# Output projections in two passes of half the contraction, six of eight tiles of each pass by Strassen's seven products

## The chip, the cores and the metric

The kernel runs on one core of a Trainium2 chip. The metric is device time in microseconds (us) from the start to the end of one execution. Engines are named as in the profile: PE is TensorE (matmuls), DVE is VectorE, ACT is ScalarE, POOL is GpSimd, SP is SyncE, whose queue issues nearly all DMAs here.

## The reference

One step of a two-layer trunk on a prompt of 1024 rows and 8 sample rows, which share the weights; the kernel computes all 1032 rows as columns of one matrix. Layer 0 is HGRN2, layer 1 a causal chunked gMLP. What matters here is the output projection at each layer's end, `y`, of a contraction over D_INNER = 2048 to D_MODEL = 1024:

```python
def hgrn2_mixer(h, s0, w_in, lb, g_norm, w_out):
    ...
    o = rmsnorm(o, g_norm).reshape(B, L, D_INNER).astype(h.dtype)
    return (o * jax.nn.silu(z)) @ w_out, S

def chunk_mlp_mixer(h, w_in, ln_g, ln_b, w_sp, b_sp, w_out):
    ...
    y = (u * s * jax.nn.silu(z)) @ w_out
    return y, v_tail

    for i in range(DEPTH):
        ...
        h = h + y
        gate = jax.nn.sigmoid(rmsnorm(h, norm_ple[i]) @ w_ple_gate[i])
        h = h + gate * (p[i] @ w_ple_proj[i])
```

## The kernel before

The 1032 columns are held transposed (features on the 128 partitions) in three chunks c = 0, 1, 2 of W = 384, 384 and 264 columns. A float32 product is made of three float32r matmuls in `mm3` (L217 to L221): high part times high part, high times low, low times high. Every operand is therefore split: ACT casts the value to its high part ("hi"), and DVE or POOL subtracts that from the value ("lo"); `split` (L213) does it for data (lo at L215), `split_weights` for weights (lo at L147). In tile names, `bh` and `bl` are the hi and lo parts of the activations (in the code also `hh`, `hl`), `whi` and `wlo` those of a weight tile, `shi` and `slo` those of sums of weight quarters (`ssum`).

The output projection is `out_phase`. Its operand is the gated branch, 16 blocks of 128 rows, which the stage ahead has stored block by block in DRAM (`ozd`); its first eight blocks lie split in SBUF when the phase starts, the second eight are loaded again and split by `load_zt` (into tiles that the profile calls zh and zl). It makes eight tiles m of 128 output rows, and for each tile and chunk one PSUM group (`ps_o`) over all 16 blocks, in two halves hf of eight (`out_half`). `add` then has DVE add the group to the residual h (L911, rows `hr[c][m]`, called h in the profile), ACT square it, and POOL sum the squares for the next normalisation (L255). The residual is loaded two tiles ahead (`load_h`, L878).

Weights come in the order of the list `order`; `take` hands out a tile and has `load` prepare the next, so that a weight tile is cast and subtracted one ahead.

Layer 1's input projection (between the two phases) already uses Strassen's form in `unit`: two weight tiles of 128 output rows against chunks 0 and 1, contraction split in two, are 2 x 2 quarters on either side, so seven products of 4 blocks x 3 matmuls at 384 columns do for eight. `load_unit` loads the two weight tiles and builds the four sums of their quarters on POOL (L188, L190, L193, L195), each split by ACT and DVE; `mix` forms the sums and differences of the operand's quarters. Chunk 2 is done plainly within the unit (`last`). The products' results are combined by DVE from PSUM into u2, u4 and c22.

Just ahead of layer 1's output projection stands a fill: `pple` multiplies half of the per-layer embedding into PSUM groups `ps_pple`, which ACT copies (L338) to SBUF on their way to DRAM (`ppd`), while the last unit's outputs are gated and stored. Its last rows of gating are `sg` (ACT L1270, DVE L1271) and `s` (POOL L1264, the product with u).

The order of PE's work is the order of the program. DVE, ACT, POOL and SP are ordered by a scheduler from priorities (`tc.high_priority`, PRI), constraints (`tc.issue_after`) and the program's order; `tk.tick()` advances side processes (normalisation, mixing) between groups of matmuls. A scratch tile named `tmp` has four buffers.

Of the kernel before, what the change touches and what calls it, by code (L numbers as in the profile page):

```python
# [17 lines left out]
P = 128  # L18
# [14 lines left out]
ZQ = 7  # L33
FDEL = ((2, 2), (2, 2), (1, 3))
# [46 lines left out]
def trunk_kernel(ctx, tc, xT, st, pT, nrm, wina, lbl, gna, wouta, winb, lng, lnb, lngr, lnbr,  # L81
# [38 lines left out]

    order = [("p", 0, 0)]
    for h in range(NH):
# [3 lines left out]
    half_order = [(m, f) for q in range(0, KT, 2) for m, f in  # L126
                  (((q, 0), (q + 1, 0), (q, 1), (q + 1, 1)) if q == 0 else
                   ((q, 0), (q, 1), (q + 1, 0), (q + 1, 1)))]
    order += [("oa", m, f) for m, f in half_order]
# [6 lines left out]
    order += [("ob", m, f) for m, f in half_order]  # L136
# [25 lines left out]
    def load(n, wait=False):  # L162
        if n >= len(order) or n in loaded or wait and order[n][0] == "B":
            return
        if order[n][0] == "B":
            loaded[n] = load_unit(order[n][1])
# [7 lines left out]
    def load_unit(m):  # L174
# [8 lines left out]
        for i in range(2):  # L183
            nc.sync.dma_start(a[i], winb[m + i])
# [161 lines left out]
    def load_zt(zt, parts, stage, n=2, lag=0, tie=True):  # L346


        todo = [(c, k0, k) for c, k0 in parts for k in range(0, zt[c, k0][2], n)]
        stg = []  # L350
        def fetch(i):
            if i < len(todo):
                c, k0, k = todo[i]
                stg.append(stage(W[c]))
                last["zt"] = nc.sync.dma_start(stg[i], ozd[c][:, k0 + k:k0 + k + n, :])

        for i in range(len(todo) + lag):
            if not lag:
                fetch(i)
            if i >= lag:  # L360
                c, k0, k = todo[i - lag]
                zh, zl, _ = zt[c, k0]
                hi = A.copy(zh[:, k:k + n, :], stg[i - lag])
                if tie:
                    tc.keep_in_program_order(hi)
                V.tensor_tensor(zl[:, k:k + n, :], stg[i - lag], zh[:, k:k + n, :].bitcast(F32), ALU.subtract)
# [15 lines left out]
    def out_half(ps, wt, zt, c, hf):  # L382
        for k in range(8):
# [3 lines left out]
                hf == 0 and k == 0, hf == 1 and k == 7)  # L387
# [461 lines left out]
    sA.close()  # L849

# [16 lines left out]
    def out_phase(key, zt, ssq, first, done, pre, parts, late, fill=None):  # L867

        with ExitStack() as s:
            st = stage2(pool(s, "zstg"), 3)  # L870
            zp = pool(s, "oz")

            def load_h(m):
                if m < KT:
                    src = xT[:, m] if first else hd[m]
                    with tc.issue_after(last["zt"].ins):
                        for c in CH:
                            nc.sync.dma_start(hr[c][m], src[:, OFF[c]:OFF[c] + W[c]])  # L878

            for c, k0, nk in parts:  # L880
                zt[c, k0] = (zp.tile([P, nk, W[c]], F32R, name=f"zh{c}_{k0}"),
                             zp.tile([P, nk, W[c]], F32R, name=f"zl{c}_{k0}"), nk)
            if fill:

                to = itertools.cycle([hr[c][m] for c in (2, 0) for m in range(4)])
                more = load_zt(zt, late[0], one(lambda: next(to)), 1, 8)
                todo = load_zt(zt, late[1], st, 2, 3)
                for gen, n in ((more, 8), (todo, 3)):
                    for _ in range(n):
                        next(gen)  # L890
                for _ in fill:
                    tk.tick()
                for _ in range(8):
                    next(more)
                run(todo)
                run(more)
            else:
                run(load_zt(zt, late, st, tie=False))
            for m in range(4):
                load_h(m)  # L900
# [4 lines left out]
            def half(ps, wt, c, hf):  # L905
                for _ in out_half(ps, wt, zt, c, hf):
                    tk.tick()

            def add(m, c, ps):
                with tc.high_priority(offset=PRI if m == KT - 1 else 0):  # L910
                    V.tensor_tensor(hr[c][m], hr[c][m], ps[:, :W[c]], ALU.add)  # L911
                accum_sq(sp, ssq[c], hr[c][m], m == 0, m == KT - 1, W[c])
                if m == KT - 1:
                    done(c)


            wt = pre["w"] if pre else take(key, 0, 0)
            for c in CH:
                if c not in pre:
                    pre[c] = bank()  # L920
                    half(pre[c], wt, c, 0)
            wt = take(key, 1, 0)
            pre1 = [pp.tile([P, 384], F32, name="ps_o1", tag=t, bufs=1) for t in ("pA", "po", "pt")]
            for c in CH:
                half(pre1[c], wt, c, 0)
            for m, pm in ((0, pre), (1, pre1)):
                wt = take(key, m, 1)
                for c in CH:
                    half(pm[c], wt, c, 1)
                    add(m, c, pm[c])  # L930
            for m in range(2, KT):
                wts = [take(key, m, hf) for hf in range(2)]
                load_h(m + 2)
                for c in CH:
                    ps = bank()
                    for hf in range(2):
                        half(ps, wts[hf], c, hf)
                    add(m, c, ps)
# [41 lines left out]
    act = new_act()  # L980
# [454 lines left out]
```

## Time and profile before

| | us |
|---|---|
| median of 3 runs (lowest to highest) | 1914.62 (1912.47 to 1915.26) |
| the profiled execution | 1914.28 |
| its span in the profile | 1912.4 |
| PE busy | 1882.9 |
| DVE, ACT, POOL busy | 1156.3, 800.1, 432.8 |
| first output projection, first to last matmul on `ps_o` | 766.45 to 947.96, 181.51 long |
| second | 1620.94 to 1802.45, 181.51 long |

The span is what the profile covers of one execution; the 1.9 us between it and the execution's time lie outside. The mean granted clock of PE is 0.993. Busy times of different engines overlap: PE's says how much of the span is matmul, the others' say how full the engines are that feed it.

### The profile page before, as it was taken

To read this page: it belongs to the slowest core of one execution; us is meant where nothing else is said; L and a number is where in the kernel's file an instruction comes from. 1 tells how busy PE (TensorE), PEld (TensorE's weight loads), DVE (VectorE), ACT (ScalarE), POOL (GpSimd) and SP (SyncE) were. 2 spreads that over 40 slices of the span, in tenths; PEclk is the share of its full clock that TensorE was granted. 3 is DMA by queue.
4 is the path that set the end of the run, shared out by engine and by line. 5 is a ranking of instruction groups with operands and counts; after the bars stand their busy time and mean duration, and the time that the engine had idled before them with its cause. 6 is when DMAs were issued, how large, how long until landed. Compare 5 with 4: busy or idle time off the path is not lost.

```text
span 1912.4 us, 33713 instructions
## 1 busy us (share of the span) xinstructions
PE 1882.9 (98%) x13250; PEld 1856.2 (97%) x13250; DVE 1156.3 (60%) x2610; ACT 800.1 (42%) x1711; POOL 432.8 (23%) x441
## 2 busy tenths in 40 slices
PE   9999999999999999999999999999999999999997
PEld 8999999999999998999999999999999999999997
DVE  5967676766767677411465755577777776311455
ACT  6463544444454546311244544434434335311342
POOL 4110000000010001011233332345445451011321
PEclk8999999999999999999999999999999999999998
DMA  6231323222231326711243343323333236611123
GB/s 214 76 117 61 118 72 103 78 81 78 92 99 60 111 69 191 251 49 51 76 143 117 109 145 99 90 81 106 124 114 106 97 108 197 222 45 45 67 89 111
DMA packets 124302, 203.76 MB, mean 107 GB/s; under 512 B 11568, under 2 KB 97264, under 8 KB 123120
## 3 DMA queue, kind: packets, MB, share of 16 engines
q1 hardware_dynamic: 124144, 201.61, 32.2%
q8 instruction: 104, 1.70, 0.4%
q14 instruction: 54, 0.44, 0.1%
HBM read 148.75 MB, written 52.82 MB: 105 GB/s over the span
## 4 chain that ended last, share of the span: by engine, by line
PE 90%; DVE 5%; DMA 2%; POOL 1%; ACT 1%; issue 1%; SPq 0%; DVEq 0%; ACTq 0%; POOLq 0%
PE ps_proj L219 18%; PE ps_proj L221 18%; PE ps_proj L220 18%; PE ps_o L219 6%; PE ps_o L220 6%; PE ps_o L221 6%; PE ps_d L221 1%; PE ps_d L219 1%; PE ps_d L220 1%; PE psp L1255 1%; PE pC L672 1%; PE pt_o L718 1%; PE p L638 1%; PE pt_g L1061 1%; PE pss L269 1%
## 5 line engine op out<-in xcount | busy, mean ns | idle before, releaser
L219 PE MATMUL ps_proj<-bh,whi 128*128 128x384 f32 (+1 forms) x2160 | 695.1, 322 | 2.1 <-ACT pple_t L338 1.6
L221 PE MATMUL ps_proj<-bh,wlo 128*128 128x384 f32 (+1 forms) x2160 | 679.9, 315 | 0.5 <-DVE wlo L147 0.5
L220 PE MATMUL ps_proj<-bl,whi 128*128 128x384 f32 (+1 forms) x2160 | 678.8, 314 | 1.4 <-POOL bl L215 1.4
L219 PEld LDWEIGHTS ps_proj<-bh,whi 128*128 128x128 f32 x2160 | 407.4, 189 | 3.6 <-ACT pple_t L338 1.7
L220 PEld LDWEIGHTS ps_proj<-bl,whi 128*128 128x128 f32 x2160 | 407.8, 189 | 2.6 <-POOL bl L215 2.6
L221 PEld LDWEIGHTS ps_proj<-bh,wlo 128*128 128x128 f32 x2160 | 406.5, 188 | 1.7 <-DVE wlo L147 1.7
L147 DVE TENSOR_TENSOR wlo<-wstg,whi 128x1024 fp32r<-128x1024 f32 x148 | 184.8, 1249 | 147.4 <-ACT whi L146 146.2
L146 ACT CAST whi<-wstg 128x1024 fp32r<-128x1024 f32 x148 | 155.0, 1048 | 155.2 <-PE ps_proj L220 104.1
L255 POOL TENSOR_TENSOR ssq<-ssq,tmp 128x384 f32<-128x384 f32 (+1 forms) x72 | 76.3, 1060 | 406.7 <-ACT tmp L254 359.9
L911 DVE TENSOR_TENSOR h<-h,ps_o 128x384 f32<-128x384 f32 (+1 forms) x48 | 24.6, 512 | 192.4 <-PE ps_o L221 190.9
L254 ACT ACTIVATE tmp<-h 128x384 f32<-128x384 f32 (+1 forms) x72 | 35.3, 491 | 219.3 <-DVE h L911 168.9
L219 PE MATMUL ps_o<-bh,whi 128*128 128x384 f32 (+1 forms) x384 | 122.1, 318 | 0.0
L220 PE MATMUL ps_o<-bl,whi 128*128 128x384 f32 (+1 forms) x384 | 121.8, 317 | 0.0
L221 PE MATMUL ps_o<-bh,wlo 128*128 128x384 f32 (+1 forms) x384 | 121.8, 317 | 0.0
L146 ACT CAST shi<-ssum 128x512 fp32r<-128x512 f32 x88 | 54.6, 622 | 110.0 <-PE ps_proj L220 60.2
L219 PE MATMUL ps_o<-zh,whi 128*128 128x384 f32 (+1 forms) x288 | 90.1, 313 | 0.0
L220 PE MATMUL ps_o<-zl,whi 128*128 128x384 f32 (+1 forms) x288 | 89.7, 312 | 0.0
L221 PE MATMUL ps_o<-zh,wlo 128*128 128x384 f32 (+1 forms) x288 | 89.7, 312 | 0.0
L215 POOL TENSOR_TENSOR ql<-q,qh 128x384 fp32r<-128x384 f32 (+1 forms) x24 | 22.4, 931 | 254.5 <-ACT qh L214 254.5
L147 DVE TENSOR_TENSOR slo<-ssum,shi 128x512 fp32r<-128x512 f32 x88 | 68.8, 783 | 12.0 <-ACT shi L146 12.0
L675 DVE TENSOR_TENSOR q<-q,t 128x192 f32<-128x192 f32 (+1 forms) x144 | 47.4, 330 | 44.7 <-PE pC L672 38.3
L219 PEld LDWEIGHTS ps_o<-bh,whi 128*128 128x128 f32 x384 | 72.2, 188 | 0.0
(303 smaller groups left out, 3930.5 us busy)
## 6 DMA issues: line engine op xcount, KB each, us to landing
wstg<-in_wina SPq DMA_DIRECT2D x48, 512.0 KB, 3.7
wstg<-in_winb SPq DMA_DIRECT2D x48, 512.0 KB, 3.7
pj<-ppd SPq DMA_DIRECT2D x16, 516.0 KB, 5.2
S<-in_st SPq DMA_DIRECT2D x16, 512.0 KB, 5.4
vb<-vd SPq DMA_DIRECT2D x16, 512.0 KB, 4.6
out_so_s<-S SPq DMA_DIRECT2D x16, 512.0 KB, 3.4
wstg<-in_wouta SPq DMA_DIRECT2D x16, 512.0 KB, 3.5
wstg<-in_wgate SPq DMA_DIRECT2D x16, 512.0 KB, 3.5
```

The lines of the kernel that those rows point to most:

```text
L146: A.copy(hi, src)
L147: V.tensor_tensor(lo, src, hi.bitcast(F32), ALU.subtract)
L215: last["lo"] = eng.tensor_tensor(lo, src, hi.bitcast(F32), ALU.subtract)
L219: PE.matmul(ps, wh, xh, start=first, stop=False, skip_group_check=more)
L220: PE.matmul(ps, wh, xl, start=False, stop=False, skip_group_check=more)
L221: PE.matmul(ps, wl, xh, start=False, stop=last, skip_group_check=more)
L254: A.activation(sq[:, :w], src, AF.Square)
L255: eng.tensor_tensor(ssq, ssq, sq[:, :w], ALU.add)
L269: PE.matmul(pss[:, i:i + 1], t[:, o:o + P], ones[:, 0:1], start=j == 0, stop=j == len(parts) - 1)
L638: PE.matmul(blk(p0, i), blk(Y, i), blk(X, i), start=True, stop=True)
L675: V.tensor_tensor(ql[:, :, 1, :], ql[:, :, 1, :], t2[:, :, 0:1].broadcast_to([P, n, lv]), ALU.mult)
L911: V.tensor_tensor(hr[c][m], hr[c][m], ps[:, :W[c]], ALU.add)
```

## The change

In both layers `out_phase` now makes two passes f = 0, 1, each over half of the contraction (8 blocks, 2 x 4). In pass 0 tiles 0 and 1 are done plainly and tiles 2 to 7 in three Strassen units, in pass 1 tiles 0 to 5 in three units and 6 and 7 plainly. So each tile is added to the residual twice: after pass 0 (`add(..., False)`: by DVE where the result is in PSUM, by POOL where it is in SBUF) and after pass 1 (`add(..., True)`, always DVE, with the squares). `unit` and `load_unit` are made general for it, `out_half` is left to single half groups.

What the passes need beside the products:

- `mix_first` forms the sums of the first half's quarters: the raw rows come back from `ozd` into the residual's tiles and four scratch tiles (`raw`, the buffers of `tmp`), DVE and POOL mix them in place, ACT and DVE or POOL split them into t1, t2, t3 (and t4, into b12's place, once the plain tiles no longer need that).
- `mix_second` does the mixing of the second half during the units (0, 2) and (0, 4), and stores the sums raw in DRAM (`tdr`).
- `jobs` brings the second half's operands in during the units (0, 6) and (1, 0), each piece into the place of one that is used up: 36 pieces of one block (four each of the quarters b11, b21, b22 and of the sums t1 to t4, eight of chunk 2; b12 follows in the unit (1, 4)), over seven buffers (three `zr`, four `raw`), hi by ACT, lo alternately by DVE and POOL. The order is b11, t2, b21, c2, t1, t3, b22, t4.
- In layer 1 the residual's tiles hold raw rows at the phase's start, so the fill's results go through the buffers of u2, u4, c22 and ssum instead, and chunk 2's pieces are reloaded through `zr`, `raw` and `sql`.

The cut diff:

```diff
+    def out_order(l):
+        return ([("o" + l, m, 0) for m in range(2)] + [("O" + l, m, 0) for m in range(2, KT, 2)] +
+                [("O" + l, m, 1) for m in range(0, KT - 2, 2)] + [("o" + l, m, 1) for m in range(KT - 2, KT)])
...
-    order += [("oa", m, f) for m, f in half_order]
+    order += out_order("a")
...
+    def load_list(todo, stage, lag=0, tie=True, engines=(V,), behind=False):
...
+                _, zh, zl, _ = todo[i - lag]
+                with tc.issue_after(rest["u2"].ins) if behind else ExitStack():
+                    hi = A.copy(zh, stg[i - lag])
...
+                engines[i % len(engines)].tensor_tensor(zl, stg[i - lag], zh.bitcast(F32), ALU.subtract)
...
+    def mix_rows(b11, b12, b21, b22, eng=V):
+
+        V.tensor_tensor(b11, b12, b11, ALU.subtract)
+        eng.tensor_tensor(b12, b22, b12, ALU.subtract)
+        V.tensor_tensor(b22, b22, b11, ALU.subtract)
+        V.tensor_tensor(b21, b21, b22, ALU.subtract)
...
+            def mix_first():
+                for j in range(4):
+                    mix_rows(*rows[j], G)
+                    for n, t in (("t2", rows[j][3]), ("t1", rows[j][0]), ("t3", rows[j][1])):
+                        split(b[n][0][:, j, :], b[n][1][:, j, :], t, G if n == "t3" else V)
...
+            def add(m, c, src, end):
+                eng = V if end or src.space == PSUM else G
+                with tc.high_priority(offset=PRI if end and m >= KT - 2 else 0):
+                    eng.tensor_tensor(hr[c][m], hr[c][m], src[:, :W[c]], ALU.add)
+                if end:
+                    accum_sq(sp, ssq[c], hr[c][m], c not in seen, m == KT - 1, W[c])
...
+            def mix_second():
+                for j in range(4):
+                    t = [raw() for _ in range(4)]
+                    quarters(8 + j, t)
+                    yield
+                    with tc.issue_after(rest["sum"].ins):
+                        mix_rows(*t)
+                    for n, x in zip(("t1", "t3", "t4", "t2"), t):
+                        nc.sync.dma_start(tdr[n][:, j, :], x)
...
+                todo = quarter("b11") + quarter("t2") + quarter("b21")
+                todo += [(ozd[2][:, 8 + k, :], b["c2"][0][:, k, :], b["c2"][1][:, k, :], W[2]) for k in range(8)]
+                todo += quarter("t1") + quarter("t3") + quarter("b22") + quarter("t4")
+                turns = itertools.cycle([zr] * ZR + [lambda w: raw()[:, :w]] * 4)
+                return load_list(todo, lambda w: next(turns)(w), ZR + 4, False, (V, G), True)
...
+                    elif (f, m) == (0, KT - 2):
+                        assert next(mixer, None) is None
+                        gen = jobs()
+                        steps(gen, ZR + 4)()
+                        then = {2: 4, 3: 4, 4: 4, 5: 8, 6: 4, 7: 4}
+                    elif (f, m) == (1, 0):
+                        then = {3: 4, 4: 4}
...
+        place = itertools.cycle([(up, n, 2, 384) for n in ("u2", "u2", "u4", "u4", "c22", "c22")] + [(ws[0], "ssum", 2, 512)] * 2)
```

A unit (f, m) has, in this order: for its first weight tile chunk 2 if `early`, then the products a11 b11, s2 t2, a12 b21, s1 t1, s3 t3, s4 b22, a22 t4, and chunk 2 of the other tile.

How the order of instructions moves. On ACT, in the fill ahead of layer 1's output projection (`sg` gates, `whi` is a weight tile, `ps_pple` the fill's groups), before:

```order
L1270 ACTIVATE sg<-u_18693 128x384 [waits DVE_49]
L146 CAST whi<-wstg 128x1024 [waits PE_49,Activation_49]
L1270 ACTIVATE sg<-u_18607 128x384 [waits DVE_49]
L338 COPY h_4_18791<-ps_pple 128x384 [waits DVE_49,PE_49]
L338 COPY h_5_18792<-ps_pple 128x384 [waits PE_49]
L338 COPY h_6_18793<-ps_pple 128x384 [waits PE_49]
```

and after:

```order
L1391 ACTIVATE sg<-u_19103 128x384 [waits DVE_49]
L149 CAST whi<-wstg 128x1024 [waits PE_49,Activation_49]
L341 COPY pple_t<-ps_pple 128x384 [waits PE_49,Activation_49,Pool_49]
L1391 ACTIVATE sg<-u_19017 128x384 [waits DVE_49]
L341 COPY pple_t<-ps_pple 128x384 [waits PE_49]
L341 COPY pple_t<-ps_pple 128x384 [waits PE_49,Pool_49]
```

The first copy now stands ahead of the last `sg` and waits for POOL, where before all three stood behind it.

On DVE, within layer 0's output projection, before, where three adds of one tile and two weight tiles' lo parts follow each other:

```order
L911 TENSOR_TENSOR h_3_10158<-h_3_10158,ps_o 128x384 [waits DMAHW0_49,PE_49]
L911 TENSOR_TENSOR h_3_10166<-h_3_10166,ps_o 128x384 [waits PE_49]
L147 TENSOR_TENSOR wlo<-wstg,whi 128x1024 [waits DVE_49,DMAHW2_49,PE_49,Activation_49]
L911 TENSOR_TENSOR h_3_10174<-h_3_10174,ps_o 128x264 [waits PE_49]
L147 TENSOR_TENSOR wlo<-wstg,whi 128x1024 [waits DMAHW3_49,DVE_49,Activation_49]
```

and after, in the last unit of pass 0, where pieces of the reload (`bl` from `raw` and `zr`) stand among the unit's sums (`u`, `c`) and the next unit's weight sums (`slo`):

```order
L373 TENSOR_TENSOR bl_125<-raw,bh_122 128x264 [waits DMAHW6_49,Activation_49]
L930 TENSOR_TENSOR u_11063<-ps_proj,u_10963 128x384 [waits DVE_49,PE_49]
L150 TENSOR_TENSOR slo<-ssum,shi 128x512 [waits Activation_49]
L373 TENSOR_TENSOR bl_125<-zr,bh_122 128x264 [waits DMAHW0_49,Activation_49]
L373 TENSOR_TENSOR bl_125<-raw,bh_122 128x264 [waits DMAHW2_49,Activation_49]
L937 TENSOR_TENSOR c_11094<-ps_d,u_11063 128x384 [waits DVE_49,PE_49]
L150 TENSOR_TENSOR slo<-ssum,shi 128x512 [waits Activation_49]
```

The unit's own sum c, on which PE's next product into the same bank waits, has reload pieces and a weight sum ahead of it.

On POOL, before, in the same phase, where only sums of squares stand:

```order
L255 TENSOR_TENSOR ssq_10182<-ssq_10182,tmp 128x384 [waits PE_49,Activation_49,Pool_49]
L255 TENSOR_TENSOR ssq_10183<-ssq_10183,tmp 128x384 [waits Activation_49]
L255 TENSOR_TENSOR ssq_10184<-ssq_10184,tmp 128x264 [waits Activation_49]
L255 TENSOR_TENSOR ssq_10182<-ssq_10182,tmp 128x384 [waits Activation_49,Pool_49]
```

and after, at the end of the reload, in unit (1, 0):

```order
L373 TENSOR_TENSOR bl_124<-raw,bh_121 128x384 [waits DMAHW1_49,PE_49,Activation_49]
L191 TENSOR_TENSOR ssum<-wstg 128x512 [waits DMAHW3_49]
L196 TENSOR_TENSOR ssum<-wstg_11190,wstg 128x512 [waits Pool_49]
L193 TENSOR_TENSOR ssum<-ssum,wstg_11190 128x512 [waits DVE_49]
L373 TENSOR_TENSOR bl_124<-raw,bh_121 128x384 [waits DMAHW4_49,PE_49,Activation_49]
```

The last piece of t4, the lowest row, stands behind three sums for the next unit's weights.

More of the change, by code (lines that the diff above doesn't have):

```diff
@@ L849, in trunk_kernel @@
     sA.close()
+    tx = pool(ctx, "mix")
+    xm = [(tx.tile([P, 4, 384], F32R, name=f"xmh{i}"), tx.tile([P, 4, 384], F32R, name=f"xml{i}")) for i in range(3)]
     hd = [dram.tile([P, T], F32, name=f"hd{m}") for m in range(KT)]
@@ L931, in out_phase @@
[L931 to L938, printed above, removed]
+                add(1, c, plain(pp.tile([P, 384], F32, name="ps_o1", tag=("pA", "po", "pt")[c], bufs=1), wt, c), False)
+                if c == 1:
+                    while any(p[2].__name__ == "mix_first" for p in tk.procs):
+                        tk.tick()
+                    b["t4"] = b.pop("b12")
+                    for j in range(4):
+                        split(b["t4"][0][:, j, :], b["t4"][1][:, j, :], rows[j][2])
+                    for m in (2, 3):
+                        load_h(m)
```

349 lines of the change are left out of this document (203 added, 146 removed).

## The prediction

> **What bounds the kernel now.** I read the busy shares first, then the chain that ended last:
>
> ```profile
> PE 1882.9 (98%) x13250; PEld 1856.2 (97%) x13250; DVE 1156.3 (60%) x2610; ACT 800.1 (42%) x1711; POOL 432.8 (23%) x441
> PE 90%; DVE 5%; DMA 2%; POOL 1%; ACT 1%; issue 1%; SPq 0%; DVEq 0%; ACTq 0%; POOLq 0%
> ```
>
> TensorE carries 90% of the chain, so a matmul removed is time removed, unless its successor then waits. The changed stages are the two output projections. The view of busy time by stretch, cut where ps_o is written (columns: length, PE, PEld, DVE, ACT, POOL, granted clock, DMA share, GB/s):
>
> ```profile
> 766.45:947.96 181.51, 181.51 (x1172) 181.51 (x1171) 48.80 (x65) 40.24 (x60) 25.92 (x23) 1.00 0.29 95
> 1620.94:1802.45 181.51, 181.51 (x1172) 181.51 (x1171) 49.59 (x74) 41.27 (x69) 25.90 (x23) 1.00 0.31 102
> ```
>
> In both, PE never idles and has its full clock, while DVE is busy 27% and POOL 14%: what the change gives these two has room on average. Whether it has room at its place is the question. Last, the timeline gives the spacing of matmuls, first in a Strassen product of today's layer 1, then at 264 columns:
>
> ```profile
> 1256.51 0.33 PE L219 MATMUL ps_d<-xmh,shi 128*128 128x384 f32 x1
> 1258.42 0.33 PE L221 MATMUL ps_d<-xmh,slo 128*128 128x384 f32 x1
> 1258.59 0.33 PE L219 MATMUL ps_proj<-bh,shi 128*128 128x384 f32 x1
> 763.60 0.28 PE L219 MATMUL ps_pple<-bh,whi 128*128 128x264 f32 x1
> 763.72 0.28 PE L220 MATMUL ps_pple<-bl,whi 128*128 128x264 f32 x1
> ```
>
> Twelve matmuls take 2.08 us, 0.1735 each; at 264 columns 0.12. A unit is 7 products and 48 narrow matmuls, 84 x 0.1735 + 48 x 0.121 = 20.4 us.
>
> **1. Products: -25.0 us.** Six units a layer, twelve in all, each with 7 products for 8: 12 x 2.08. The loads go with their matmuls (13250 of each), so they do not take over as the bound. The adds into h double, but those from PSUM fall on a DVE with 73% idle.
>
> **2. The fill ahead of layer 1's projection: -3 (0 to -5.3).** PE idles here today:
>
> ```profile
> 1611.15 0.44 PE L219 MATMUL ps_pple<-bh,whi 128*128 128x384 f32 x1 [3.84 <-ACT h L338]
> 1612.73 0.52 PE L220 MATMUL ps_pple<-bl,whi 128*128 128x384 f32 x1
> 1613.05 0.52 PE L221 MATMUL ps_pple<-bh,wlo 128*128 128x384 f32 x1
> 1609.16 0.52 ACT L1270 ACTIVATE sg<-u 128x384 f32<-128x384 f32 x1 [2.23 <-DVE u L1182]
> 1610.62 1.24 ACT L338 COPY h<-ps_pple 128x384 f32<-128x384 f32 x3 [0.94 <-DVE sg L1271]
> 1606.04 1.27 POOL L1264 TENSOR_TENSOR s<-s,u 128x384 f32<-128x384 f32 x1 [2.42 <-DVE s L1258]
> ```
>
> The three copies that free the banks start at 1610.62, behind the last sg; then matmuls come at 0.32 until 1615.6, ten of them 0.15 late each (1.5 us). After, the first copy stands ahead of that sg and waits only for POOL's last product (1606.04 + 1.27 = 1607.3): its bank is free near 1607.8, the second after sg, near 1610.1. Two waits of 0.65 and 1.3 us remain for some 4.0: 2.05 saved, and the slow stretch with it if such short waits leave the clock alone, 3.55; I take 3. The ends are nothing, and the whole 3.84 + 1.5.
>
> **3. Mixing at layer 0's start: +2 (0 to 4.8).**
>
> ```profile
> 769.44 0.35 SPq L160 DMA_DIRECT2D wstg<-in_wouta  x1
> wstg<-in_wouta SPq DMA_DIRECT2D x16, 512.0 KB, 3.5
> L219 PE MATMUL ps_o<-zh,whi x288: 281/334/422, 788.9 to 1798.6; 128*128 128x384 f32 x80, 128*128 128x264 f32 x64
> L948 DVE TENSOR_TENSOR h<-h,tmp 128x384 f32<-128x384 f32 x32 | 17.8, 556 | 0.9
> L215 DVE TENSOR_TENSOR vl<-pt_v,vh 128x384 fp32r<-128x384 f32 x32 | 17.6, 550 | 0.7
> L215 DVE TENSOR_TENSOR bl<-tmp,bh 128x384 fp32r<-128x384 f32 x24 | 20.5, 856 | 1.2 <-ACT bh L214 1.2
> L147 DVE TENSOR_TENSOR slo<-ssum,shi 128x512 fp32r<-128x512 f32 x88 | 68.8, 783 | 12.0 <-ACT shi L146 12.0
> 1121.18 0.69 DVE L147 TENSOR_TENSOR slo<-ssum,shi 128x512 fp32r<-128x512 f32 x1
> L215 POOL TENSOR_TENSOR ql<-q,qh 128x384 fp32r<-128x384 f32 x16 | 16.4, 1026 | 196.6 <-ACT qh L214 196.6
> L215 POOL TENSOR_TENSOR bl<-tmp,bh 128x384 fp32r<-128x384 f32 x24 | 29.5, 1233 | 26.3 <-ACT bh L214 26.2
> 1114.88 1.29 POOL L188 TENSOR_TENSOR ssum<-wstg 128x512 f32<-128x512 f32 x1 [1.98 <-DMA wstg<-in_winb]
> L190 POOL TENSOR_TENSOR ssum<-ssum,wstg 128x512 f32<-128x512 f32 x22 | 29.2, 1328 | 80.4 <-DVE slo L147 80.4
> ```
>
> These lines price everything added on DVE and POOL. Tiles 0 and 1 end where the second half begins today, 788.9; the first unit starts with 24 narrow matmuls (2.9) and a11 b11 (2.08), and wants the last quarter of t2 1.6 later, at 795.5. The second weight tile, if issued as today's at 769.44, lands at 772.9. Then stand on DVE four slo 0.69, a wlo 1.22, twelve mixings and eight lo parts 0.55, 15.0 us; on POOL four sums 1.29 and seven of 1.03, 12.4. Side by side at the loaded prices (0.86, 0.78) DVE needs 17.9, to 790.8: no wait. One after the other, 27.4, to 800.3: 4.8 late. What decides is whether the two run at once, and layer 0's own normalisation shows them meet:
>
> ```profile
> 1060.91 1.22 DVE L147 TENSOR_TENSOR wlo<-wstg,whi 128x1024 fp32r<-128x1024 f32 x1
> 1061.32 1.68 POOL L215 TENSOR_TENSOR bl<-h,bh 128x384 fp32r<-128x384 f32 x1 [0.97 <-ACT bh L214]
> 1062.05 1.36 DVE L215 TENSOR_TENSOR bl<-h,bh 128x384 fp32r<-128x384 f32 x1
> ```
>
> POOL's 1.02 became 1.68, ending at 1063.0; DVE's 0.55 became 1.36, ending 0.4 after it. Alone the three are 2.80, here 2.50 from start to end: nearly in turn, at 0.90 of the sum. So I stand between the ends, +2.
>
> By the Trainium skill, "SBUF — State Buffer", section "Who interferes with whom", a DVE instruction with two SBUF inputs and a GpSimd instruction that reads SBUF exclude each other, and the second fully blocks. The three rows agree, but for the 0.90. By it in full this term is 4.8 instead of 2.
>
> **4. Layer 1's start: +2 (0 to 4.4).** Chunk 2's pieces and sixteen quarters are reloaded behind the last store of ozd:
>
> ```profile
> 1611.50 0.32 SPq L1273 DMA_DIRECT2D ozd<-s  x1
> 790.11 6.55 SPq L878 DMA_DIRECT2D h<-in_xT  x12
> h<-in_xT SPq DMA_DIRECT2D x16, 192.0 KB, 3.9
> ```
>
> An issue takes 6.55 / 12 = 0.55: 24 of them (three stores and five pieces ahead of the quarters) end at 1624.7, the first four quarters land near 1622. From there 21 operations of 0.55 on DVE (twelve mixings, a copy, eight lo parts) and 8 of 1.03 on POOL, 19.8 in turn, reach 1641.8, and with adds and a wlo that stand behind them the first unit's weight is ready near 1644.3. PE wants it at 1639.9 (today's start at 1620.94 less the 3.5 of term 2, and 22.5 for tiles 0 and 1, 96 x 0.1735 + 48 x 0.121). Side by side DVE needs 14.0 and is in time.
>
> **5. The pass change: +4 per layer, +8 (0 to 11.3 each).** The largest doubt. While the last unit of pass 0 and the first of pass 1 run, 36 pieces of second-half operands come back, each in the place of one whose last product has just ended. The window runs from the first free operand to the last quarter of t4 in unit (1, 0): 15.4 left of one unit and 17.0 of the next, 32.4 us. In it POOL has 14 lo parts of 384 (1.03), 4 of 264, 5 weight sums (1.29) and 3 adds into h (1.03):
>
> ```profile
> L215 POOL TENSOR_TENSOR bl<-tmp,bh 128x264 fp32r<-128x264 f32 x12 | 9.9, 837 | 7.2 <-ACT bh L214 7.2
> L147 DVE TENSOR_TENSOR wlo<-wstg,whi 128x1024 fp32r<-128x1024 f32 x148 | 184.8, 1249 | 147.4 <-ACT whi L146 146.2 <-PE psp L1255 0.4
> L911 DVE TENSOR_TENSOR h<-h,ps_o 128x384 f32<-128x384 f32 x32 | 17.7, 554 | 176.2 <-PE ps_o L221 174.7 <-DMA h<-hd 1.5
> ```
>
> 14.4 + 3.4 + 6.5 + 3.1 = 27.4. DVE has 18 lo parts (at most 0.55), five slo and 2.5 wlo (1.25 at most): 16.4. Strictly in turn 43.8, which is 11.4 late. At loaded means POOL alone needs 31.0 (1.23, 0.84, 1.33), DVE 22.5: in time by 1.4. With the 0.90 of the rows above 39.4, and of this the 3.1 of wlo may fall later: 36.3, some 4 late. It shows at two places: the sum c22, which on DVE stands behind reload pieces, before a22 t4 of unit (0, 6); and t4's last piece, on POOL behind three sums of the next unit.
>
> **6. Clock: +3 (0 to 9).** A wait of 2.35 us elsewhere was followed by half clock (third last column, 0.50):
>
> ```profile
> 751.74 0.49 PE L718 MATMUL pt_o<-ident,on 128*128 128x128 f32 x2 [2.35 <-DVE ss_e L712]
> 752.00:755.40 3.40, 3.40 (x14) 3.31 (x13) 3.06 (x8) 2.97 (x9) 0.37 (x1) 0.50 0.89 240
> ```
>
> Six waits are possible (each layer's start, and two at each pass change); I let two be that long, at the 1.5 us of the fill.
>
> By the Trainium skill, "TensorE: Matmul & The Clock Gate", Part 1, the array goes cold after an idle window of about 3.4 us. By it waits of 2 us cost nothing more, and the sum would be 3 lower, 1899.6. The trace has half clock after a shorter one, and I go by the trace.
>
> **7. Other units: +1**, 0.1 for each of ten; today's Strassen units run without a gap in this stretch (22.24 us of PE in 22.24):
>
> ```profile
> 1224.88:1247.12 22.24, 22.24 (x150) 22.13 (x148) 12.32 (x31) 9.86 (x19) 7.03 (x6) 1.00 0.33 95
> ```
>
> Sum: -25.0 - 3 + 2 + 2 + 8 + 3 + 1 = -12.0. The profiled run took 1914.28 (span 1912.4 and 1.9 around it), so 1902.3; the median, 1914.62, is 0.3 higher: 1902.6.
>
> **Rivals.** (a) *Everything hides.* DVE and POOL overlap as their means suggest; terms 3 to 6 vanish: 1914.6 - 25 - 3 + 1 = 1887.6, with the whole fill gone 1885.3. For it speaks the busy share of 27% and 14%; against it the three rows. Chance 0.27. (b) *Exclusion in full, slower.* DVE and POOL strictly in turn at the pass changes: 2 x 11.4 + 4.8 + 4.4 + 9 + 1 - 28 = +14, 1928.6. With the starts and the clock at their ends the kernel gets slower than before by 0.2% once a pass change costs more than 6.5 us. For it the rows of exclusion; against it the loaded means, in which most pairs do overlap in part. Chance 0.22, of which 0.13 slower and 0.09 within 0.2%. (c) *Transfers.* 29 pieces go round 7 buffers, each landing, cast and subtracted: 29 / 7 x (3.9 + 1.6) = 22.8 us of 32.4, hidden. The largest loads take 6.2:
>
> ```profile
> xs<-in_xT SPq DMA_DIRECT2D x8, 384.0 KB, 6.2
> ```
>
> That would just fit; at 8 us a pass change is 7.4 late, 6.8 more in all, 1909. Chance 0.05. That fewer matmuls might not be issued faster is excluded by equal counts of loads and matmuls.
>
> **Numbers.** The forecast, 1895 to 1911, has 0.46. A measurement here tells 0.2%, 3.8 us. Faster than 1910.8: 0.46 + 0.27, the forecast's upper edge outweighed by most of (c): 0.73; slower than 1918.4: 0.13 of (b) and 0.01 of (c); within: the other 0.09 of (b) and 0.04 at that edge. The range, 1885 to 1917, takes in (a) whole and the lower part of (b).
>
> **What would show it.** PE's instructions fall by 144 matmuls, ps_o and ps_proj products keep 0.1735 between them; PE idle ahead of products of unit (0, 6) and (1, 0) named after bl on POOL or c22 on DVE, some 4 us a layer, is right for term 5; none there means (a), 10 or more means (b), waits on a DMA (c). Idle before the fill's third group near 2 us is right for term 2. If PE waits in units between, on u or slo, none of my terms holds it and I am wrong.

## The result and the profile after

The changed kernel takes 1928.81 us (median, 1927.21 to 1932.36), the kernel before 1914.42 beside it: slower, ratio 1.0079 (95% interval 1.0062 to 1.0097). Forecast were 1902.6 and a range that ended at 1917. Medians here are of the fast runs; one run of e4 and one of e18, below, took more than twice as long and is left out.

The busy shares and the chain that ended last, of the profiled execution after (span 1928.5, before 1912.4):

```profile
PE 1870.2 (97%) x13106; PEld 1840.3 (95%) x13106; DVE 1329.4 (69%) x2841; ACT 865.7 (45%) x1855; POOL 586.9 (30%) x563
PE 77%; DVE 8%; DMA 7%; issue 3%; POOL 2%; ACT 2%; SPq 1%; DVEq 0%; ACTq 0%; POOLq 0%
```

PE has its 144 matmuls less, and its share of the chain fell from 90% to 77%: PE now waits. The view by stretch tells where. First the first output projection, the fill and the second output projection of before, then the same three of after (length, PE, PEld, DVE, ACT, POOL, clock, DMA share, GB/s; each from its first matmul to the first of the next stage):

```profile
766.45:948.08 181.63, 181.63 (x1173) 181.63 (x1171) 48.92 (x65) 40.24 (x60) 25.93 (x23) 1.00 0.29 95
1604.01:1620.94 16.93, 13.09 (x74) 12.77 (x73) 8.59 (x16) 7.02 (x15) 1.27 (x1) 0.90 0.64 202
1620.94:1802.56 181.62, 181.62 (x1172) 181.62 (x1171) 49.70 (x74) 41.27 (x69) 25.90 (x23) 1.00 0.31 102
```
```profile
768.05:958.76 190.71, 176.86 (x1101) 174.71 (x1099) 134.41 (x182) 73.58 (x133) 103.83 (x83) 0.96 0.52 171
1614.45:1627.14 12.69, 11.56 (x73) 11.24 (x73) 7.97 (x14) 6.55 (x14) 1.27 (x1) 1.00 0.72 231
1627.14:1817.95 190.81, 175.53 (x1100) 173.57 (x1099) 134.40 (x188) 73.87 (x138) 103.46 (x83) 0.96 0.51 165
```

A projection took 181.6 and takes 190.7 and 190.8, 9.1 longer each, where 72 matmuls of 0.1735 less would make it 12.5 shorter: 21.6 us in each, 43 together, went into waits and slow clock. The fill gave back 4.2. The 2 us that remain of the 16.1 lie outside these stages. DVE's busy time in the first went from 48.9 to 134.4, POOL's from 25.9 to 103.8.

What PE waited for, the main rows of the view of waits (us in total, times, the longest), in 760 to 965 and then in 1600 to 1820:

```profile
PE ps_d L222 <- DVE c L937: 8.8, 3, 5.2
PE ps_proj L223 <- DVE xml L218: 2.3, 1, 2.3
PE ps_proj L222 <- ACT xmh L217: 2.1, 1, 2.1
...
PE ps_d L222 <- DVE c L937: 12.5, 4, 6.8
PE ps_proj L224 <- DVE wlo L150: 1.4, 1, 1.4
```

The waits inside the two projections add to 29.1 us. Nearly three quarters of them, 21.3, are waits for c, the sum c22, which must have read the bank before the unit's last product, a22 t4, adds into it. In unit (0, 6) they are 5.24 and 6.75 us, in (1, 0) 2.16 and 3.2. The other three, 1.40, 1.04 and 1.51, lie in (0, 2) and (0, 4). The first of the long waits on PE, and DVE's timeline ahead of it (start, duration; two pieces in the row x2):

```profile
864.19 0.69 PE L222 MATMUL ps_d<-bh,whi 128*128 128x384 f32 x1 [5.24 <-DVE c L937]
```
```profile
855.21 1.38 DVE L373 TENSOR_TENSOR xml<-zr,xmh 128x384 fp32r<-128x384 f32 x1
856.51 1.36 DVE L373 TENSOR_TENSOR bl<-zr,bh 128x384 fp32r<-128x384 f32 x1
857.80 0.42 DVE L1036 TENSOR_TENSOR h<-h,ps_proj 128x264 f32<-128x264 f32 x1
858.14 1.92 DVE L373 TENSOR_TENSOR bl<-raw,bh 128x384 fp32r<-128x384 f32 x2
859.98 0.55 DVE L930 TENSOR_TENSOR u<-ps_proj,u 128x384 f32<-128x384 f32 x1
860.55 0.82 DVE L150 TENSOR_TENSOR slo<-ssum,shi 128x512 fp32r<-128x512 f32 x1
861.29 0.97 DVE L373 TENSOR_TENSOR bl<-zr,bh 128x264 fp32r<-128x264 f32 x1
862.18 1.49 DVE L373 TENSOR_TENSOR bl<-raw,bh 128x264 fp32r<-128x264 f32 x1
863.59 0.54 DVE L937 TENSOR_TENSOR c<-ps_d,u 128x384 f32<-128x384 f32 x1
```

DVE is busy throughout. Six lo parts of the reload and a weight sum's (slo) stand ahead of c, and those of 384 columns take up to 1.38 instead of 0.55; u, on which c depends, is late with them.

### The profile page after: what moved, and what is told of

It is laid out like the page before. It is cut to its first block, busy times and chain, and to the rows that moved or that the text cites. A ratio compares the mean times of both kernels' runs of the same rounds, so it can differ in the third digit from the quotient of the medians.

```text
span 1928.5 us, 34355 instructions
## 1 busy us (share of the span) xinstructions
PE 1870.2 (97%) x13106; PEld 1840.3 (95%) x13106; DVE 1329.4 (69%) x2841; ACT 865.7 (45%) x1855; POOL 586.9 (30%) x563
## 4 chain that ended last, share of the span: by engine, by line
PE 77%; DVE 8%; DMA 7%; issue 3%; POOL 2%; ACT 2%; SPq 1%; DVEq 0%; ACTq 0%; POOLq 0%
PE ps_proj L222 19%; PE ps_proj L224 19%; PE ps_proj L223 19%; PE ps_d L222 2%; PE ps_d L224 2%; PE ps_d L223 2%; DMA raw<-ozd 1%; PE psp L1376 1%; PE pC L679 1%; DVE wlo L150 1%; PE pt_o L725 1%; PE pss L272 1%; DMA dt<-raw 1%; PE p L645 1%; PE ps_o L222 1%
## 5 line engine op out<-in xcount | busy, mean ns | idle before, releaser
L222 PE MATMUL ps_proj<-bh,whi 128*128 128x384 f32 (+1 forms) x2448 | 784.7, 321 | 4.1 <-ACT pple_t L341 1.6
L224 PE MATMUL ps_proj<-bh,wlo 128*128 128x384 f32 (+1 forms) x2448 | 768.8, 314 | 3.1 <-DVE wlo L150 2.8
L223 PE MATMUL ps_proj<-bl,whi 128*128 128x384 f32 (+1 forms) x2448 | 767.4, 313 | 2.2 <-POOL bl L218 2.2
L222 PEld LDWEIGHTS ps_proj<-bh,whi 128*128 128x128 f32 x2448 | 464.2, 190 | 6.4 <-ACT pple_t L341 1.7
L223 PEld LDWEIGHTS ps_proj<-bl,whi 128*128 128x128 f32 x2448 | 464.4, 190 | 2.9 <-POOL bl L218 2.9
L224 PEld LDWEIGHTS ps_proj<-bh,wlo 128*128 128x128 f32 x2448 | 462.7, 189 | 4.5 <-DVE wlo L150 4.5
L222 PE MATMUL ps_proj<-xmh,shi 128*128 128x384 f32 x248 | 84.3, 340 | 2.4 <-ACT xmh L217 2.1
L223 PE MATMUL ps_proj<-xml,shi 128*128 128x384 f32 x248 | 83.4, 336 | 2.3 <-DVE xml L218 2.3
L224 PE MATMUL ps_proj<-xmh,slo 128*128 128x384 f32 x248 | 83.2, 336 | 0.0
L1385 POOL TENSOR_TENSOR s<-s,u 128x384 f32<-128x384 f32 (+1 forms) x48 | 53.1, 1106 | 68.9 <-DVE s L1379 68.3
```

Source lines behind the costliest of these rows:

```text
L222: PE.matmul(ps, wh, xh, start=first, stop=False, skip_group_check=more)
L223: PE.matmul(ps, wh, xl, start=False, stop=False, skip_group_check=more)
L224: PE.matmul(ps, wl, xh, start=False, stop=last, skip_group_check=more)
L1385: G.tensor_tensor(s[:, :w], s[:, :w], us[mm, c][:, :w], ALU.mult)
```

## The experiments

Theories: A, DVE and POOL exclude each other and have too much to do in turn; B, the reload's transfers and buffers; C, no exclusion, DVE alone is overfull; D, what stands ahead of c in DVE's queue holds it; E, the weights of the units to come stand behind the reload on SP's queue.

**What costs how much: parts left out.** e3 leaves out the second half's mixing and the reload, e5 only the reload, e11 of the reload all but its transfers, e2 its lo parts; e12 keeps the work and leaves out the transfers.

```diff
e3  -mixer = mix_second(); next(mixer)
    +mixer = iter(())
e3, e5  -gen = jobs()    -gen = load_list(quarter("b12", "t1"), ...)
        +gen = iter(())  (both)
e2, e11: in load_list, no subtraction / neither cast nor subtraction for the 36 pieces
e12  -stg.append(stage(todo[i][3]))
     +stg.append(hr[0][2][:, :todo[i][3]])      (and no dma_start)
```

> The changed kernel without the second half's mixing, its stores, and the whole reload (left out: pass 1 works on the operands of pass 0). What is left of the change is the products, the first half's mixing, the adds and the new fill. Both theories: all waits behind the first unit go; left are those at the two starts, 5.6 and 2.6 us with 2 of slow clock: 1914.4 - 25 - 4 + 10, 1893 to 1899. Above 1905 the products would be worth less than 25 us, or the adds and the unit itself cost what I gave 1 us.

> The changed kernel with the second half's mixing (its loads, sums and stores) but without the reload of 36 pieces a layer and of b12 (left out: pass 1 works on the operands of pass 0). Between e3_no_second (1896.8) and the changed kernel (1928.8) it splits the 32 us. Theory A (exclusion at the pass change alone): the mixing costs next to nothing, 1897 to 1899. Theory D (DVE's queue is in order: an instruction that waits for a transfer holds the sum c behind it): the mixings that wait for raw quarters hold c in units (0, 2) and (0, 4), 1.6 us in layer 0, 1.2 and 1.7 in layer 1, with slow clock: 1901 to 1905.

> The changed kernel with the 36 reload transfers a layer, and neither the hi casts nor the lo parts behind them (left out: pass 1 works on the operands of pass 0). e2_hi_only (casts and transfers) stands at 1913.9, e5_no_reload (neither) at 1903.0. If the transfers by themselves cost the 10.9 us between (the next unit's weights stand behind them on SP's queue and land late): 1909 to 1914. If it is ACT's queue, in which casts that wait for a piece hold the weights' casts: 1903 to 1906.

> The changed kernel without the lo parts of the reload of 36 pieces a layer at the pass change (left out: the lo operands of pass 1 stay those of pass 0); transfers, buffers and the hi casts on ACT stay. Theory A: DVE and POOL lose the work that makes c22 late; the waits of the pass change (17.4 us in both layers, with some 6 of slow clock) all but vanish: 1903 to 1908. Theory B (transfers and buffers): the waits stay, 1923 to 1929. If both bear, it lies between, and tells their shares.

> The changed kernel with all casts and lo parts of the reload, but made from rows that lie in SBUF, without the 36 transfers a layer (left out: the operands of pass 1 are not those of the second half). Theory A (work on DVE and POOL): the waits of the pass change stay, 1924 to 1929. Theory B (transfers and their buffers): they mostly go, 1908 to 1916. Between, it gives the share of the transfers in the presence of the lo parts.

Measured: e3 1896.75, e5 1902.96, e11 1914.42, e2 1913.88, e12 1921.78 (before 1913.2 to 1914.3 beside them). The two projections of e3:

```profile
765.55:941.99 176.44, 172.13 (x1101) 171.04 (x1100) 99.71 (x146) 56.54 (x93) 79.86 (x63) 0.98 0.32 107
1609.09:1784.30 175.21, 171.51 (x1101) 170.80 (x1099) 101.69 (x152) 56.89 (x98) 79.74 (x63) 0.99 0.30 102
```

Of these, by idle time and granted clock, some 7.3 and 5.2 are waits and slow clock at the starts (an estimate), so about 169 and 170 are left of 181.6: the products are worth nearly their 25 us. Then 6.2 us are the second mixing, 11.5 the transfers by themselves, nothing the casts, 14.9 the lo parts. Work without transfers costs 18.8 over e5, transfers without work 11.5, both together 25.9: two causes, of which each hides a little of the other. e2 and e12 lie between the ranges expected, as they must where both causes bear.

They lie at different places. The waits of PE for c at the pass change of layer 0 (840 to 895, units (0, 6) and (1, 0)), without transfers and with transfers alone:

```profile
866.22 0.69 PE L222 MATMUL ps_d<-bh,whi 128*128 128x384 f32 x1 [6.63 <-DVE c L938]
```
```profile
878.05 0.69 PE L222 MATMUL ps_d<-bh,whi 128*128 128x384 f32 x1 [5.50 <-DVE c L937]
```

Without transfers the wait is in (0, 6), 6.63 us (5.5 in layer 1), and none is in (1, 0) of layer 0, a small one in layer 1; with transfers alone it is in (1, 0), 5.50 (2.7 in layer 1), and none in (0, 6). With the casts (e2) PE waits only 1.17 and 0.75 us for c in (1, 0), but c itself is as late: in layer 0 it starts 112.7 us after the projection's first matmul, in e11 113.0. There it is PE that comes later, by waits and slow clock ahead of that place. The chain ahead of the wait in (1, 0) of e11, on SP, POOL and DVE:

```profile
863.49 1.32 SPq L362 DMA_DIRECT2D raw<-dt  x3
864.86 0.43 SPq L187 DMA_DIRECT2D wstg<-in_wouta  x1
...
870.99 1.28 POOL L191 TENSOR_TENSOR ssum<-wstg 128x512 f32<-128x512 f32 x1 [12.13 <-DMA wstg<-in_wouta]
...
872.96 1.09 DVE L150 TENSOR_TENSOR slo<-ssum,shi 128x512 fp32r<-128x512 f32 x1 [8.96 <-ACT shi L149]
...
877.46 0.54 DVE L937 TENSOR_TENSOR c<-ps_d,u 128x384 f32<-128x384 f32 x1
```

The weights of unit (1, 2) are issued at 864.86, behind reload pieces, and land 6 us later; POOL sums them, ACT and DVE split the sums, and since that split stands ahead of u and c of unit (1, 0) in DVE's queue, DVE idles 8.96 us and PE waits, with no piece to blame. In the changed kernel itself these weights are issued at 874.48 and DVE idles only 1.52 us for their split, with lo parts of the reload around it; how much of its 2.16 and 3.20 us in (1, 0) is due to the weights no run tells.

**Exclusion.** e1 has DVE make all lo parts of the reload, e4 all mixing and lo parts at the start, e8 both, e13 also pass 0's adds from SBUF (on e10, below).

```diff
e1  -load_list(todo, ..., ZR + 4, False, (V, G), True)
    +load_list(todo, ..., ZR + 4, False, (V,), True)
e4  -mix_rows(*rows[j], G)    ...    -split(..., t, G if n == "t3" else V)
    +mix_rows(*rows[j], V)    ...    +split(..., t, V)
e13 -eng = V if end or src.space == PSUM else G
    +eng = V
```

> The changed kernel (1928.8 us) with one thing different: DVE makes all lo parts of the operands reloaded between the passes; POOL makes none of them. Theory A (DVE and POOL exclude each other; at the pass change they work in turn, and the sum c22 comes late because the lo parts ahead of it on DVE take 1.37 instead of 0.55): 17 lo parts a layer go from 1.03 on POOL to 0.55 on DVE, 8 us a layer less in turn; the waits for c in units (0, 6) and (1, 0), now 7.4 and 10.0 us with 4 and 2 of slow clock, shrink by about half: 1912 to 1920. Theory B (the round of store, load and buffer decides): 1926 to 1931. Theory C (no exclusion, DVE alone has too much in its queue): DVE gets 17 pieces more ahead of c, 9 us a layer: 1935 to 1945.

> The changed kernel with the first half's mixing, and the lo parts of t3, wholly on DVE (4 mixings and 4 lo parts a layer leave POOL). Theory A: in turn 8 x 1.03 become 8 x 0.55, 3.8 us less at each start; the waits at the starts (5.6 and 2.6 us, with about 2 of slow clock) mostly go: 1920 to 1925. Theory C (side by side): DVE, which PE waits for there, gets 4.4 us longer a layer: 1933 to 1938.

> e1_lo_all_dve and e4_mix_dve together (all lo parts of the reload and all mixing at the start on DVE). They touch different places: if their gains add, 1928.8 - 8.6 - 5.1 = 1915, 1913 to 1917. Theory C would have DVE overloaded: 1920 or more.

> e10_mix_behind_c with the adds of pass 0 from SBUF on DVE too (9 a layer, from 1.03 on POOL to 0.55). Theory A: 4.3 us a layer less in turn, in part under cover: 1 to 6 lower than e10. If DVE's own queue is full there: no change, or up to 5 higher.

Measured: e1 1920.19 (ratio to before 1.0047, 1.0023 to 1.0071), e4 1921.53 (1.0059, 1.0039 to 1.0079), e8 1913.78 (0.9995, 0.9985 to 1.0005), e13 1921.26 where e10 has 1917.64. The intervals of e1 and e4 overlap that of the changed kernel, 1.0062 to 1.0097; that of e8, both together, is far below it. Its gain, 15.0, is about the sum of theirs, 8.6 and 7.3. In the profiles the two projections together take 381.5 us in the changed kernel, 373.5 in e1, 373.8 in e4 and 369.5 in e8. DVE has 20 operations more in a projection of e1 (202 for 182) and PE waits less, so C falls. What was expected of e4's place did not come: the waits at the starts did not mostly go, they fell from 5.0 to 3.9 and from 2.8 to 1.9 us, and the rest of its gain lies in later units and in less slow clock. The groups of lo parts on DVE in the pass change of layer 0, changed kernel (848 to 890) and then e1 (846 to 888; count, busy, mean ns):

```profile
L373 DVE TENSOR_TENSOR bl<-zr,bh 128x384 fp32r<-128x384 f32 x4 | 5.5, 1363 | 0.1
L373 DVE TENSOR_TENSOR xml<-zr,xmh 128x384 fp32r<-128x384 f32 x3 | 4.1, 1367 | 0.0
```
```profile
L373 DVE TENSOR_TENSOR bl<-zr,bh 128x384 fp32r<-128x384 f32 x9 | 5.3, 629 | 1.3 <-ACT bh L370 1.2
L373 DVE TENSOR_TENSOR xml<-zr,xmh 128x384 fp32r<-128x384 f32 x4 | 2.0, 548 | 0.0
```

The same operation takes 1363 ns with POOL at the same work and 629 without: nine pieces in the time of four. The Trainium skill, "SBUF — State Buffer", "Who interferes with whom", calls the port pair that the two engines share an exclusive lock. These rows agree in kind; strictly in turn a piece on each engine would take 0.55 + 1.03 = 1.58 us, and the means side by side are below that, so the two still overlap a little.

e13 does not fit A: moving 9 adds to the engine that does them in half the time cost 3.6 us. Its trace shows where. PE's waits for c at the pass changes fall from 17.0 us in e10 to 2.7, and 8.2 for lo parts of the reload, of which e10 has none, and 3.9 for the sum u come in their place. Why the whole got longer stays open.

**Order on DVE.** e6 puts mixing and lo parts behind c, e9 is e8 with that order, e10 is e8 with the mixing alone behind c.

```diff
-            V.tensor_tensor(c22, psd_, u4, ALU.add)
+            rest["sum"] = V.tensor_tensor(c22, psd_, u4, ALU.add)
-({4: 1}, {2: 1, 4: 1, 7: 1})
+({5: 1}, {2: 1, 5: 1, 7: 1})
e6, e9 -then = {2: 4, 3: 4, 4: 4, 5: 8, 6: 4, 7: 4}
       +then = {2: 4, 3: 4, 5: 12, 6: 4, 7: 4}      (and DVE's lo parts by issue_after(rest["sum"].ins))
```

> The changed kernel with another order on DVE alone: in a unit's second half the mixings and the reload's lo parts on DVE stand behind the sum c, not ahead of it (four pieces of the reload are taken up one product later). No work is added or taken away. Theory D (what stands ahead of c in DVE's queue makes PE wait): the waits for c in (0, 2), (0, 4) and (0, 6), 7 us in layer 0 and 9.8 in layer 1, with some 4 of slow clock, mostly go, some come back as waits for late pieces: 1912 to 1919. Theory A (the sum of DVE's and POOL's work in the window is too much): the same lateness shows at another place, 1925 to 1930.

> e8_both_dve with the order of e6_c_first. Theories A and D together: the work in turn is less and c is not behind it: 1902 to 1911. If the reload's transfers bind instead (theory B), 1913 or more.

> e8_both_dve (1913.8) with only the second half's mixing moved behind c on DVE (the reload's order is left). e6_c_first had lost the waits in (0, 2) and (0, 4) by this and more than that by the later lo parts. Theory D for the mixing: the waits of 1.4 in layer 0 and 0.5 and 1.4 in layer 1, with their slow clock, go: 1908 to 1912. If the later stores make the reload late instead: 1914 to 1918.

Measured: e6 1931.61, e9 1925.03, e10 1917.64: worse by 2.8 (within the noise), 11.3 and 3.9 than the kernels they start from, and e6 above both ranges expected. D as a remedy falls: the wait in (0, 4) of layer 0 goes, but what is put behind c is late for its own product. In e9's layer 0 PE's waits for c fall to one of 3.2 us, and seven for reload pieces and their casts appear, 5.6 us together. So the lateness at the pass change is one of amount: order moves it to another place.

**The weights' queue.** e14 (on the changed kernel), e15 and e16 (on e8) and e17 (on e11) issue the units' weights from POOL, e16 from ACT.

```diff
-            nc.sync.dma_start(a[i], winb[m + i] if f is None else wsrc[key.lower()][m + i, f])
+            (nc.sync if f is None else nc.gpsimd).dma_start(a[i], ...)      (e16: nc.scalar)
```

> The changed kernel with the weight tiles of the output projections' units issued by POOL instead of SP, nothing else. Theory E (SP's queue: the weights of unit (1, 2) stand behind reload pieces that wait for their buffers, so the sums of the weights come late, and DVE, which splits them ahead of c in unit (1, 0), holds PE): the waits in (1, 0), 2.3 and 3.4 us with some 3 of slow clock in both layers, mostly go: 1919 to 1924. If the traffic makes them land late: 1926 to 1931.

> e8_both_dve (1913.8) with the weight tiles of the units issued by POOL. Theory E: the waits for c in (1, 0), 3.6 us in each layer with some 3 of slow clock in all, go: 1903 to 1909, faster than before (1914). If the traffic makes them land late: 1912 to 1916.

> e8_both_dve with the weight tiles of the units issued by ACT. Theory E: as e15_all_weights_pool, 1903 to 1909, and up to 5 more where an issue that waits for its buffer holds ACT's casts. If the traffic makes them land late: 1912 to 1918.

> e11_transfers_only (1914.4; the 36 reload transfers a layer, casts and lo parts left out) with the weight tiles of the units issued by POOL. Theory E: the wait of 5.8 and 3.0 us in (1, 0) goes, near e5_no_reload (1903.0): 1902 to 1907. If the traffic makes them land late: 1911 to 1915.

Measured: e14 1938.88, e15 1932.59, e16 1925.60, e17 1911.85; the first three lie above every range expected. In e17 the waits of (1, 0) are gone in both layers, so E names the cause of the waits that the transfers bring there. It gained only 2.6 us in all, which is within the noise, and the waits at other units grew (at layer 1's start 3.68 us of idle where e11 has 1.98). With the lo parts in place the waits of (1, 0) stay (4.9 us in e15, layer 0), now with pieces right ahead of c. More changed than the order on SP's queue: from POOL the weights go through a queue that the page lists as q0, software_dynamic, where SP's is q1, hardware_dynamic, and the issues stand behind POOL's sums. From ACT it is q10, hardware_dynamic, and e16 lost 11.8 too. What exactly cost the time was not taken apart.

**Take the units out of pass 1.** e18 keeps pass 0 as changed (mixing and lo parts on DVE) and makes pass 1 plain: no second mixing, 24 pieces reloaded. e19 does four plain tiles and two units in pass 0.

```diff
e19 -[("o" + l, m, 0) for m in range(2)] + [("O" + l, m, 0) for m in range(2, KT, 2)] + ...
    +[("o" + l, m, 0) for m in range(4)] + [("O" + l, m, 0) for m in range(4, KT, 2)] +
    +[("o" + l, m, 1) for m in range(KT)]
    +todo = quarter("b11") + quarter("b21") + (c2, 8 pieces) + quarter("b12", "t1") + quarter("b22")
```

> Three Strassen units in pass 0 of each layer as changed, pass 1 plain for all eight tiles: no sums of the second half's quarters, no stores of them, 24 reload pieces a layer for 36, all lo parts and all mixing on DVE. Products: 6 units for 12, -12.5; fill -4.2; starts as in e4_mix_dve, +8; if theories A, D and E hold (pieces cost PE time where they meet a unit's sums and the weights of units to come), the reload costs only what falls in unit (0, 6), +2 to +4: 1905 to 1911. If the reload as such makes PE wait (pieces late for the plain tiles): 1914 or more.

> As e18_pass0_only with four plain tiles (0 to 3) ahead of two units in pass 0, which gives the mixing 22 us more before its sums are wanted. Products: 4 units, -8.3; fill -4.2; starts +0 to +2; reload +2 to +4: 1901 to 1908, faster than before (1914). If the starts' waits are not from the mixing's lateness, as much as e18_pass0_only or more.

Measured: e18 1904.28 (ratio to before 0.9957, 0.9940 to 0.9973), e19 1903.13 (0.9946, 0.9934 to 0.9958): both beat both kernels. e19's two projections:

```profile
765.23:942.73 177.50, 177.50 (x1149) 177.50 (x1148) 86.45 (x145) 54.79 (x97) 42.10 (x36) 1.00 0.39 130
1611.35:1790.60 179.25, 178.10 (x1149) 177.56 (x1147) 87.91 (x151) 56.12 (x102) 42.70 (x36) 1.00 0.37 123
```

In the first PE has no wait and its full clock: two units' 4.2 us are kept whole, with DVE at 86 us where the change had 134. In both layers e19 keeps 6.5 of 8.3 us; e18, with projections of 180.0 and 177.1, keeps 6.2 of 12.5, the rest going mostly to waits at the first unit.

## Why the prediction was wrong, by its steps

Forecast was a change of -12.0 us, and the profiled run has +16.1. Of the 28 between them 11 are term 6, 9 term 5, 4 terms 3 and 4, 3 term 7 and 2 lie outside these stages; the fill gave 1 more than forecast.

**Term 1, products, -25.0:** right, or nearly (e3).

**Term 2, the fill, -3:** right in mechanism; -4.2 was measured. The first copy stands ahead of sg, and one wait of 1.13 us is left where two of 0.65 and 1.3 were expected.

```profile
1616.66 0.47 ACT L341 COPY pple_t<-ps_pple 128x384 f32<-128x384 f32 x1
1618.98 0.52 ACT L1391 ACTIVATE sg<-u 128x384 f32<-128x384 f32 x1 [1.85 <-DVE u L950]
```

**Terms 3 and 4, the starts, +2 and +2:** at the places named, waits of 5.0 (2.06, 2.30 and 0.65) and 2.8 us (0.90, 1.37 and 0.52). The upper end for layer 0, 4.8 with DVE and POOL in turn, comes near, and a value between the ends was taken where the three rows quoted already gave nine tenths of the sum. That it fits to 0.2 us is luck in part: POOL's first weight sum begins at 775.84, not near 772.9, and five adds into h (2.6 us) that the sum left out stand in DVE's queue; PE for its part came 1.6 later, and DVE and POOL needed some 24 us for the 27.4 summed. With POOL out of the mixing (e4) 3.9 of the 5.0 us remain.

**Term 5, the pass change, +4 a layer:** this is the step that failed: the waits are 7.4 and 9.9 us. It summed DVE's and POOL's work over one window and compared it with the window's length. Three things were missing. The wlo (3.1 us) were let fall "later", but they stand ahead of u and c in the same queue (in layer 0 at 854.07 and 883.52). The window starts full and DVE can't catch up: c in unit (0, 6) comes in the middle, while much of the work is still waiting, not at the end. And the weights of unit (1, 2) were not costed on SP's queue, which the reload fills; that is a cause of its own (e11, e17), whose share in the changed kernel is open. The second place named, t4's last piece behind three sums, shows in no wait of PE in the changed kernel.

**Term 6, the clock, +3:** sized for two waits of the six thought possible. The waits that the profile gives add to 13.8 and 15.3 us in the two projections, 29 of the 43 lost; the other 14 are slow clock and the first matmuls after a wait. By the granted clock, in steps of 1 us, 11.3 of the 14 are slow clock, 8.3 of them behind the four waits of the pass changes: most of this miss follows from term 5. After 1.40 us of idle the clock stayed full, after 5.24 it was half (changed kernel, 835.40 and 864.19):

```profile
864.19:867.60 3.41, 3.41 (x11) 3.41 (x12) 3.41 (x4) 2.66 (x6) 3.41 (x4) 0.50 0.62 189
...
835.40:838.80 3.40, 3.40 (x22) 3.40 (x23) 3.37 (x5) 0.00 (x0) 1.81 (x2) 1.00 0.69 224
```

**Term 7, other units, +1:** some 4. In (0, 4) of both layers (1.40 and 1.51) mixings that wait for raw quarters stand ahead of c; in (0, 2) of layer 1 (1.04) mixings and weight splits do. The second mixing was in no term of the sum, though it adds 16 operations a layer to DVE and 32 transfers to SP; by e5 it costs 6.2 us.

**The rivals.** (b), exclusion in full, gave 1928.6, and 1928.8 was measured, at a chance of 0.22. That DVE and POOL slow each other is shown (the rows of e1, and e8), but it is not the whole of it: with no lo part in the reload at all, e2 still has 1913.9, 17 us above e3. That (b)'s sum fits is luck: it had 22.8 for the two pass changes where 17.3 were measured, 9.2 for the starts (7.8), 9 for the clock (14), 1 for other units (4) and nothing outside the stages (2). (a), everything hides, falls. (c), transfers, looked at the round of buffers, which was not where they cost: by themselves (e11) they cost by standing ahead of the weights. That made (c) too unlikely at 0.05.

What stays open: why e13, e14, e15 and e16 lost, how the changed kernel's waits in (1, 0) divide between the weights' lateness and the pieces, and how much of e10's loss is the later stores and how much the changed order of the reload behind them.

## What to carry to other kernels

When a change adds work to a side engine, an average over a window is no cover: list what stands ahead of the one instruction that the bound engine waits for, at the moment it is wanted, with every queue that feeds it, the weights' transfers included. On engines that exclude each other give an elementwise operation to the faster one alone; splitting it in two halves was slower than all of it on DVE (1928.8 against 1920.2, and with the mixing already on DVE 1921.5 against 1913.8). Saving 2.08 us of matmul a unit paid where the side work was small (pass 0) and not where the operands had to be exchanged at the same time; taking a third or half of the saving kept 6 us of it (e19, e18), and the whole kept none.

## What the runs showed of the hardware that was not expected

Half clock came after shorter waits than the 2.35 us of the prediction, and not at once after all longer ones. Two first matmuls behind a wait in e8, by the timeline, and the 3.4 us from each of them, by the view by stretch (third last column: the clock):

```profile
1705.93 0.67 PE L222 MATMUL ps_d<-xmh,whi 128*128 128x384 f32 x1 [1.96 <-DVE c L937]
...
855.35 0.44 PE L222 MATMUL ps_d<-bh,whi 128*128 128x384 f32 x1 [3.15 <-DVE c L937]
```
```profile
855.35:858.75 3.40, 3.40 (x12) 3.40 (x13) 3.40 (x5) 2.06 (x6) 2.04 (x2) 0.60 0.80 231
...
1705.93:1709.30 3.37, 3.37 (x11) 3.37 (x12) 3.37 (x5) 2.17 (x5) 2.03 (x2) 0.51 0.80 237
```

After 1.96 us of idle the first matmul is already slow (0.67) and the clock is 0.51; after 3.15 it is fast (0.44), and the clock falls later, to a mean of 0.60.

The Trainium skill, "TensorE: Matmul & The Clock Gate", Part 1, has the array go cold after an idle window of about 3.4 us, in windows that run freely. The traces differ in the first part: 1.96 us of idle sufficed here. That the start of the slow stretch varies agrees with free windows, though no run here shows the windows themselves.

The view of DMAs in 848 to 890 of the changed kernel gives the landing of one weight tile of 512 KB, issued at 875.91:

```profile
wstg<-in_wouta SPq DMA_DIRECT2D x3, 512.0 KB, 5.9
```

With the reload's transfers alone (e11) one issued at 865.86 took 6.7 us, without the reload (e5) one issued at 845.7 took 3.8, and the page of before has a median of 3.5. With one tile each this suggests, and does not show, that the reload's traffic slows the very transfer that stands behind it.
